# Reading the stationary weights with a step of two elements in a float32r encoder trunk

## The chip, the cores and the metric

The kernel runs on 1 core of one Trainium2 chip. The metric is device microseconds of that core for one execution; shorter is better. The time before is the median of three runs.

## The reference

Two residual layers over one sequence of 256 tokens, 2048 channels, all in float32. Layer 0 mixes tokens by a gated MLP (gMLP), layer 1 by grouped-query attention with 16 heads; after each stands a gated feed-forward with a three-tap convolution. Every part is normed and modulated by a conditioning vector c. Cut to the products that matter here:

```python
mod = silu(c) @ w_ada[i] + b_ada[i]              # 6 vectors of 2048 a layer: "ada"
h = rmsnorm(x) * (1 + sc1) + sh1
# layer 0                                        # layer 1
u, v = split(gelu(h @ w_in))                     # q, k, v = split(h @ w_qkv)
y = (u * spatial(rmsnorm(v))) @ w_out            # y = attention(q, k, v) @ w_o
x = x + gt1 * y
h = rmsnorm(x) * (1 + sc2) + sh2
g, val = split(conv3(h @ w_up))                  # w_up: 2048 x 11264
x = x + gt2 * ((gelu(g) * val) @ w_down)         # w_down: 5632 x 2048
```

## The kernel before

Activations lie transposed: channels on the 128 partitions, the 256 tokens along the free dimension. A float32 product is made of three float32r products: each operand is split into a part hi (its value cast to float32r) and a part lo (the rest), and hi x hi, hi x lo and lo x hi are summed in PSUM (`prod_b`, L204 to 208).

`weight` (L175 to 199 with its inner function) loads up to 128 x 2048 weights into a raw tile by one DMA from SP's queue, casts each half of 1024 columns into a tile hi on ScalarE (L185) and subtracts it into a tile lo on VectorE (L186). It gives back a function `cols(c, n)`, which returns the slices of hi and lo that hold the columns c to c + n. There are five raw, five hi and five lo buffers.

Most products use a weight block of 128 x 128 as the stationary operand (lhsT) and 256 tokens as the moving one, one weight load to each matmul: pu (`w_in`, u half) and po (`w_out`) in layer 0, pw (`w_o`) in layer 1, and in both layers pfa, pfc and pf (`w_up`, in three arrays) and pd (`w_down`). They call `cols` with n = 128. In pu, pfa, pfc and pf the moving operand is a slice of the tiles hhi and hlo (the normed input, all 16 channel blocks in one tile); in po, pw and pd it is a tile fhi or flo of its own for each block. The products pv (`w_in`, v half), pk and pq (`w_qkv`) are turned round: 512 weight columns move, and a block of hhi or hlo is stationary.

The conditioning vectors are made on VectorE alone: 192 column blocks of w_ada, each 1 MB from DRAM, each one multiply-and-sum of 128 x 2048 (L137). A queue deals them out among the weights at a rate set for each stage (`pump`), most of them in layer 0 and in the attention; the feed-forward of layer 1 has none behind its first part.

A scheduler sets the order of instructions on each engine. On the host, `_layout` puts each weight array into DRAM in the order in which it is read: a row of a partition holds the blocks of 128 columns side by side.

Of the kernel before, what the change touches and what calls it, by code (L numbers as in the profile page):

```python
# [15 lines left out]
P = 128  # L16
# [30 lines left out]
def kernel(  # L47
# [21 lines left out]
        return cur["ps"].tile([P, 512], F32, tag=tag or cur["tag"], name=name, bufs=cur["bufs"][tag or cur["tag"]])  # L69

    def phase(stack, name, nf, bufs={"ps": 8}, tag="ps", rt="ps"):
        """pools that live for one mixer: PSUM banks, split activations, scratch"""
        cur["ps"] = stack.enter_context(tc.tile_pool(name=name + "_ps", bufs=1,
                                                     space=bass.MemoryType.PSUM, reuse_waits="tile"))
        cur["bufs"], cur["tag"], cur["rt"] = bufs, tag, rt
        cur["f"] = stack.enter_context(tc.tile_pool(name=name + "_f", bufs=nf, reuse_waits="tile"))
        cur["scr"] = stack.enter_context(tc.tile_pool(name=name, bufs=1, reuse_waits="tile"))
        return cur["scr"]
# [1 line left out]
    def raw_tile(name):  # L80
        return raws.tile([P, 2048], F32, tag="raw", name=name)

# [1 line left out]
    def small(name, shape, src=None):  # L84
        t = const.tile(shape, F32, tag=name, name=name)
        if src is not None:
# [7 lines left out]
    x = const.tile([P, NB, S], F32, tag="x", name="x")  # L94
# [13 lines left out]
    mod = small("mod", [P, DEPTH, 6 * NB])  # L108
    gs = small("gs", [P, DEPTH * 2, NB])

# [1 line left out]
    cond = small("cond", [P, NB])  # L112
    A.activation(cond, cT, AF.Exp, scale=-1.0)
    V.tensor_scalar(out=cond, in0=cond, scalar1=1.0, scalar2=None, op0=ALU.add)
# [14 lines left out]
        A.copy(cond_bc[:, b * S:(b + 1) * S], pb[:, :S])  # L129
    c_st.close()  # L130

# [1 line left out]
    def ada(l, vec, j):  # L133
        m = vec * NB + j
        w = raw_tile(f"ada{l}_{m}")
# [21 lines left out]
        while it not in done:  # L157
            pump_one()

# [1 line left out]
    cnt = [0]  # L161
    pend = []

# [11 lines left out]
    def weight(src, ncol):  # L175
        pump()
        cnt[0] += 1
        w = raw_tile(f"w{cnt[0]}")
        Q.dma_start(w[:, :ncol], src)
        his_, los_ = [], []  # L180
        for c in range(0, ncol, HW):
            n = min(HW, ncol - c)
            hi = his.tile([P, HW], F32R, tag="hi", name=f"hi{cnt[0]}_{c}")
            lo = los.tile([P, HW], F32R, tag="lo", name=f"lo{cnt[0]}_{c}")
            A.copy(hi[:, :n], w[:, c:c + n])  # L185
            V.tensor_tensor(out=lo[:, :n], in0=w[:, c:c + n], in1=hi[:, :n].bitcast(F32), op=ALU.subtract)  # L186
            his_.append(hi)
            los_.append(lo)

        ready = list(pend)  # L190
        pend.clear()
        for fn in ready:
            fn()

        def cols(c, n):
            k, o = divmod(c, HW)
            return his_[k][:, o:o + n], los_[k][:, o:o + n]

        return cols
# [7 lines left out]
        mm(out, whi, xlo, False, False)  # L207
        mm(out, wlo, xhi, False, stop)

# [1 line left out]
    accs = {}  # L211

    def square_into(name, j, src):
# [1 line left out]
            square_(name, j, src)  # L215

    def square_(name, j, src):
        """sum of squares over the blocks of x, two blocks at a time; the last block goes to the tensor engine"""
        if j < NB - 2 and j % 2 == 0:
            return  # L220
        if j < NB - 2:
            src, n = x[:, j - 1:j + 1, :].rearrange("p j t -> p (j t)"), 2 * S
        else:
            n = S
        if j == 1:
            accs[name] = tmp.tile([P, 2 * S], F32, tag="acc", name=f"acc_{name}", bufs=1)
            A.activation(accs[name], src, AF.Square)
            return
        s = tmp.tile([P, 2 * S], F32, tag="sqj", name=f"sq_{name}{j}", bufs=SQB)[:, :n]
        A.activation(s, src, AF.Square)  # L230
        if j < NB - 1:
            V.tensor_tensor(out=accs[name][:, :n], in0=accs[name][:, :n], in1=s, op=ALU.add)
        else:
            a = accs[name]
            accs[name] = (a[:, S:], a[:, :S], s)

    def rstd_bcast(name, keep):
        """1 / rms of every token over all partitions: a PSUM tile, and a copy in SBUF if it is kept for long"""
        pm = bank(f"pm_{name}", cur["rt"])
        r = tmp.tile([P, TC], F32, tag="r", name=f"r_{name}")  # L240
        dg = tmp.tile([P, S], F32, tag="ht", name=f"dg_{name}")
        pr = bank(f"pr_{name}", cur["rt"])
        for i, a in enumerate(accs[name]):
            for t in range(TC):
                T.matmul(pm[:, t:t + 1], lhsT=a[:, t * P:(t + 1) * P], rhs=mean_w, start=i == 0 and t == 0,
                         stop=i == 2, skip_group_check=True)
        with tc.high_priority():
            V.tensor_scalar(out=r, in0=pm[:, :TC], scalar1=EPS, scalar2=None, op0=ALU.add)
            G.tensor_tensor(out=r, in0=r, in1=neghalf[:, :TC], op=ALU.pow)
            for t in range(TC):  # L250
                V.tensor_scalar(out=dg[:, t * P:(t + 1) * P], in0=ident, scalar1=r[:, t:t + 1],
                                scalar2=None, op0=ALU.mult)
                T.matmul(pr[:, t * P:(t + 1) * P], lhsT=ones, rhs=dg[:, t * P:(t + 1) * P], start=True, stop=True)
            if not keep:
                return pr[:, :S]
            R = cur["scr"].tile([P, S], F32, tag="R", name=f"R_{name}", bufs=1)
            A.copy(R, pr[:, :S])
        return R
# [32 lines left out]
            V.scalar_tensor_tensor(out=x[:, j, :], in0=src, scalar=mcol(l, vec, j), in1=x[:, j, :],  # L291
                                   op0=ALU.mult, op1=ALU.add)

# [1 line left out]
    def gmlp(l, rstd):  # L295
        with ExitStack() as st:
            gm = phase(st, "gm", NB)
# [87 lines left out]
    def gqa(l, rstd):  # L385
        with ExitStack() as st:
            at = phase(st, "at", NH, {"pa": 2, "pq": 2, "pb": 4}, "pb", "pq")
# [18 lines left out]
            for kb in range(NB):  # L406
                w = weight(wqkv0_d[kb], 1536)
# [7 lines left out]
                        mm(pk[t][n], hlo[:, kb, ts_], w(n * 512, 512)[0], False, kb == NB - 1)  # L415

            def rope(nm, ps2, cs):
                """un-normalised rotation of four heads and 1/rms of each; ps2: banks per t-chunk"""
                ss = at.tile([P, TC * 4], F32, tag="qss", name=f"ss{cs}", bufs=2)
                rot = [at.tile([P, 512], F32, tag="p", name=f"rot{cs}{t}", bufs=PB) for t in range(TC)]  # L420
                for t in range(TC):
                    src = ps2[t]
                    for h in range(4):
                        s = at.tile([P, P], F32, tag="qsq", name=f"qsq{cs}{t}{h}", bufs=2)
                        A.activation(s, src[:, h * P:(h + 1) * P], AF.Square,
                                     accum_out=ss[:, t * 4 + h:t * 4 + h + 1])
                    s4 = src.rearrange("p (h d) -> p h d", h=4)
                    V.tensor_tensor(out=rot[t].rearrange("p (h d) -> p h d", h=4), in0=s4,
                                    in1=tabs[nm + "c"][:, t:t + 1, :].broadcast_to([P, 4, P]), op=ALU.mult)
                    sw = at.tile([P, 512], F32, tag="sw", name=f"sw{cs}{t}", bufs=1)  # L430
                    s5 = src.rearrange("p (h a c f) -> p h a c f", h=4, a=2, c=2)
                    sw5 = sw.rearrange("p (h a c f) -> p h a c f", h=4, a=2, c=2)
                    t5 = tabs[nm + "s"][:, t, :].rearrange("p (a c f) -> p a c f", a=2, c=2)
                    for c in range(2):
                        V.tensor_tensor(out=sw5[:, :, :, c, :], in0=s5[:, :, :, 1 - c, :],
                                        in1=t5[:, :, c, :].unsqueeze(1).broadcast_to([P, 4, 2, 32]), op=ALU.mult)
                    V.tensor_tensor(out=rot[t], in0=rot[t], in1=sw, op=ALU.add)
                V.tensor_scalar(out=ss, in0=ss, scalar1=1.0 / P, scalar2=EPS, op0=ALU.mult, op1=ALU.add)
                G.tensor_tensor(out=ss, in0=ss, in1=neghalf, op=ALU.pow)
                return rot, ss  # L440
# [91 lines left out]
            for half in range(2):  # L532
                for j2 in range(NB // 2):
                    w = weight(wo_d[half, j2], 2048)
# [16 lines left out]
    def ffn(l, rstd, nxt, defer):  # L551
        with ExitStack() as st:
# [7 lines left out]
                return b[:, :S], b[:, S:]  # L560

            def epilogue(i, src):
                """three-tap convolution along the tokens of both halves, then gelu(g) * val, split"""
                t = ff.tile([P, 2 * S], F32, tag="t", name=f"t{l}_{i}", bufs=2)
                cols = (i, NPAIR + i)
                for a, o, n in zip(src, halves(t), cols):
# [70 lines left out]
            for pi, nk in enumerate(PARTS):  # L637
# [11 lines left out]
                for j in range(NB):  # L649
                    off = base * NB * P + j * nk * P  # L650
                    w = weight(wdn_d[l, :, off:off + nk * P], nk * P)
# [49 lines left out]


def _cols(a, *lead):
    """(..., n*128) -> [128, ..., n]"""
    n = a.shape[-1] // P
    a = a.reshape(*a.shape[:-1], n, P)
    return np.moveaxis(a, -1, 0)


def _nblock(w):  # L710
    """(K, N) -> [N/128][128 k][K/128, 128 n]: the blocks of one column block side by side"""
    K, N = w.shape
    return w.reshape(K // P, P, N // P, P).transpose(2, 1, 0, 3).reshape(N // P, P, -1)


def _rope_tables():
# [11 lines left out]
def _layout(inp):  # L728
    a = {k: np.asarray(v) for k, v in inp.items()}
    o = {}  # L730
# [28 lines left out]
    parts, b = [], 0  # L759
    for nk in PARTS:  # L760
        parts.append(dn[:, b:b + nk].transpose(0, 2, 3, 1, 4).reshape(DEPTH, P, NB * nk * P))
        b += nk
    o["wdn"] = np.concatenate(parts, 2)
    o["ident"] = np.eye(P, dtype=np.float32)
    o["cos"], o["sin"] = _rope_tables()
    return {k: np.ascontiguousarray(v) for k, v in o.items()}
# [23 lines left out]
```

## Time and profile before

| | before |
|---|---|
| median of 3 runs | 2172.94 us (2172.78 to 2173.63) |
| profiled execution, first to last instruction | 2173.2 us |
| mean granted TensorE clock | 0.980 |
| TensorE matmul busy | 2099.9 us (97%), 16328 matmuls |
| TensorE weight load busy | 2037.8 us (94%), 16328 loads |
| VectorE busy | 1706.8 us (79%) |
| ScalarE busy | 1019.5 us (47%) |
| HBM read | 575.99 MB, 266 GB/s over the span |

The profiled execution's span is its own time; it lies 0.3 us over the median of the runs. Records of neighbouring matmuls overlap (a matmul of 256 columns has a record of about 0.28 us), so the time that a matmul takes in a stream is the distance from one start to the next, not the length of its record.

### The profile page before, as it was taken

The numbers are of one execution on the slowest core, as the hardware profiler recorded it, in microseconds if no ns is written. First come the engines' busy times: TensorE is split into PE (matmuls) and PEld (weight loads), VectorE is DVE, ScalarE is ACT, GpSimd is POOL, SyncE is SP. The second block draws the span as 40 slices with busy tenths as digits, with TensorE's granted clock in tenths as the row PEclk, the third lists the DMA queues.
The fourth block names the chain that finished last, engine by engine and source line by source line (L and its number), as shares of the span: only waits on it lengthen the run. The fifth ranks groups of instructions, "written<-read, shape, count | busy, mean of one in ns | idle before, by whom it ended". The sixth has DMA issues, their size and how long they took to land.

```text
span 2173.2 us, 39151 instructions
## 1 busy us (share of the span) xinstructions
PE 2099.9 (97%) x16328; PEld 2037.8 (94%) x16328; DVE 1706.8 (79%) x2291; ACT 1019.5 (47%) x1501; POOL 16.6 (1%) x15
## 2 busy tenths in 40 slices
PE   6889998999999999999999999899999999999997
PEld 4669998999999999999988789899999999999997
DVE  8989888889988989889985677876978566655665
ACT  3343444446544554345455554443653445434542
POOL 0000000000000000000000000000000000000000
PEclk7999999999999999999999999899999999999999
DMA  9999997885798889988976346677558655555542
GB/s 370 405 376 360 343 335 275 338 356 201 282 356 326 324 327 336 335 324 309 338 251 224 119 177 242 218 272 296 192 179 320 229 184 178 192 181 188 174 159 95
DMA packets 85137, 580.62 MB, mean 267 GB/s; under 512 B 9952, under 2 KB 11488, under 8 KB 25056
## 3 DMA queue, kind: packets, MB, share of 16 engines
q1 hardware_dynamic: 84960, 578.12, 71.6%
q8 instruction: 128, 2.10, 0.4%
q14 instruction: 49, 0.40, 0.1%
HBM read 575.99 MB, written 2.10 MB: 266 GB/s over the span
## 4 chain that ended last, share of the span: by engine, by line
PE 54%; issue 36%; DVE 7%; ACT 1%; DMA 1%; POOL 0%; SPq 0%; POOLq 0%; DVEq 0%; ACTq 0%
PE pf L202 18%; PE pd L202 11%; PE po L202 4%; PE pu L202 4%; PE pfc L202 4%; DVE ada L137 4%; PE pw L202 3%; PE pk L202 3%; PE pq L202 3%; DVE lo L186 2%; PE pfa L202 2%; PE pqo L506 1%; PE psc L477 0%; DMA ada<-in_wada 0%; ACT hi L185 0%
## 5 line engine op out<-in xcount | busy, mean ns | idle before, releaser
L185 ACT CAST hi<-w 128x1024 fp32r<-128x1024 f32 x740 | 740.1, 1008 | 929.9 <-PE pf L202 360.7
L186 DVE TENSOR_TENSOR lo<-w,hi 128x1024 fp32r<-128x1024 f32 x740 | 859.6, 1170 | 358.6 <-ACT hi L185 353.1
L202 PE MATMUL pf<-hhi_f,lo 128*128 128x256 f32 x2144 | 606.8, 283 | 0.0
L202 PE MATMUL pf<-hhi_f,hi 128*128 128x256 f32 x2144 | 606.8, 283 | 0.0
L202 PE MATMUL pf<-hlo_f,hi 128*128 128x256 f32 x2144 | 606.8, 283 | 0.0
L137 DVE CUSTOM_DVE_ANT_0 ada<-ada,cond_bc,bada 128x2048 f32<-128x2048 f32 x192 | 449.3, 2346 | 24.2 <-DMA ada<-in_wada 24.0
L202 PEld LDWEIGHTS pf<-hhi_f,hi 128*128 128x128 f32 x2144 | 411.6, 192 | 0.0
L202 PEld LDWEIGHTS pf<-hhi_f,lo 128*128 128x128 f32 x2144 | 411.6, 192 | 0.0
L202 PEld LDWEIGHTS pf<-hlo_f,hi 128*128 128x128 f32 x2144 | 411.6, 192 | 0.0
L202 PE MATMUL pd<-fhi_f,hi 128*128 128x256 f32 x1408 | 392.1, 280 | 0.0
L202 PE MATMUL pd<-flo_f,hi 128*128 128x256 f32 x1408 | 391.6, 279 | 0.0
L202 PE MATMUL pd<-fhi_f,lo 128*128 128x256 f32 x1408 | 391.2, 279 | 0.0
L202 PEld LDWEIGHTS pd<-fhi_f,lo 128*128 128x128 f32 x1408 | 264.1, 188 | 0.0
L202 PEld LDWEIGHTS pd<-fhi_f,hi 128*128 128x128 f32 x1408 | 263.6, 188 | 0.0
L202 PEld LDWEIGHTS pd<-flo_f,hi 128*128 128x128 f32 x1408 | 263.1, 187 | 0.0
L202 PE MATMUL pfc<-hhi_f,hi 128*128 128x256 f32 x448 | 126.1, 283 | 0.0
L202 PE MATMUL pfc<-hlo_f,hi 128*128 128x256 f32 x448 | 126.1, 283 | 0.0
L202 PE MATMUL pfc<-hhi_f,lo 128*128 128x256 f32 x448 | 125.5, 283 | 0.0
L570 DVE SCALAR_TENSOR_TENSOR t<-pf,cw,t 128x255 f32<-128x255 f32 x240 | 101.7, 474 | 0.0
L202 PEld LDWEIGHTS pfc<-hhi_f,hi 128*128 128x128 f32 x448 | 85.8, 192 | 0.0
L202 PEld LDWEIGHTS pfc<-hlo_f,hi 128*128 128x128 f32 x448 | 85.8, 192 | 0.0
L202 PEld LDWEIGHTS pfc<-hhi_f,lo 128*128 128x128 f32 x448 | 85.4, 192 | 0.0
(187 smaller groups left out, 2844.6 us busy)
## 6 DMA issues: line engine op xcount, KB each, us to landing
ada<-in_wada SPq DMA_DIRECT2D x192, 1024.0 KB, 6.6
w<-in_wup SPq DMA_DIRECT2D x134, 1024.0 KB, 4.8
w<-in_wdn SPq DMA_DIRECT2D x64, 1024.0 KB, 4.9
w<-in_wup SPq DMA_DIRECT2D x48, 896.0 KB, 5.5
w<-in_wdn SPq DMA_DIRECT2D x32, 768.0 KB, 4.7
w<-in_wv SPq DMA_DIRECT2D x16, 1024.0 KB, 7.1
w<-in_wu SPq DMA_DIRECT2D x16, 1024.0 KB, 7.1
w<-in_wout SPq DMA_DIRECT2D x16, 1024.0 KB, 5.3
```

Source lines behind the costliest of these rows:

```text
L137: V.tensor_tensor_reduce(out=w, in0=w, in1=cond_bc, op0=ALU.mult, op1=ALU.add, scale=1.0, scalar=bada[:, l, m:m + 1], accum_out=mod[:, l, ...
L185: A.copy(hi[:, :n], w[:, c:c + n])
L186: V.tensor_tensor(out=lo[:, :n], in0=w[:, c:c + n], in1=hi[:, :n].bitcast(F32), op=ALU.subtract)
L202: T.matmul(out, lhsT=a, rhs=b, start=start, stop=stop, skip_group_check=True)
L506: T.matmul(po, lhsT=va[:, kc, g * P:(g + 1) * P], rhs=ps_[h][:, kc, :], start=kc == 0, stop=kc == TC - 1)
L570: V.scalar_tensor_tensor(out=o[:, to], in0=a[:, frm], scalar=cw[:, l, tap, n:n + 1], in1=o[:, to], op0=ALU.mult, op1=ALU.add)
```

## The change

Two neighbouring blocks of 128 columns are laid in DRAM by turns, column 0 of the first, column 0 of the second, column 1 of the first, and so on, in all arrays whose blocks are stationary. The DMA, the cast and the subtraction treat the row as before. `cols`, asked for one block (n = 128), returns every second element of the 256 that hold the pair. Where 512 columns move (`in_wv`, `in_wqkv0`, `in_wqkv1`) nothing changes. In the built program 14976 of the 16328 weight loads read with a step of two elements instead of one; the instructions, their order and their waits are otherwise the same on every engine. Comments that went away are left out here.

```diff
@@ weight @@
         def cols(c, n):
             k, o = divmod(c, HW)
+            if n == P:
+                o, q = o // (2 * P) * (2 * P), o // P % 2
+                return [t[:, o:o + 2 * P].rearrange("p (n q) -> p q n", q=2)[:, q, :] for t in (his_[k], los_[k])]
             return his_[k][:, o:o + n], los_[k][:, o:o + n]
@@ host @@
+def _pairs(w):
+    return w.reshape(*w.shape[:-1], -1, 2, P).swapaxes(-1, -2).reshape(w.shape)
...
@@ _layout @@
     o["wdn"] = np.concatenate(parts, 2)
+    for k in ("wu", "wout", "wo", "wup0", "wup1", "wup2", "wdn"):
+        o[k] = _pairs(o[k])
```

## Rows read from the trace of the kernel before

**Rows 1.** The page: span, busy time by engine, clock in 40 slices.

```profile
span 2173.2 us, 39151 instructions
...
PE 2099.9 (97%) x16328; PEld 2037.8 (94%) x16328; DVE 1706.8 (79%) x2291; ACT 1019.5 (47%) x1501; POOL 16.6 (1%) x15
...
PEclk7999999999999999999999999899999999999999
```

**Rows 2.** Chain of waits, in order of time: start us, length us, what, matmuls.

```profile
252.47 87.52 PE po L202 x743
...
561.11 90.45 PE pd L202 x768
651.56 184.32 PE pf L202 x1536
```

**Rows 3.** Timeline of PE, 512 columns moving: start us, record us, what.

```profile
1150.43 0.39 PE L202 MATMUL pk<-lo,hhi_b 128*128 128x512 f32 x1
...
1150.88 0.39 PE L202 MATMUL pk<-lo,hhi_b 128*128 128x512 f32 x1
1151.11 0.39 PE L202 MATMUL pk<-hi,hhi_b 128*128 128x512 f32 x1
```

**Rows 4.** PE's timeline in a stretch at half clock, and its window (PEclk: granted clock).

```profile
353.88 0.41 PE L202 MATMUL pfa<-hlo_f,hi 128*128 128x256 f32 x1
354.09 0.41 PE L202 MATMUL pfa<-hhi_f,lo 128*128 128x256 f32 x1
...
354.73 0.41 PE L202 MATMUL pfa<-hhi_f,lo 128*128 128x256 f32 x1
...
core 0: us, PE busy (x) PEld busy (x) DVE busy (x) ACT busy (x) POOL busy (x), PEclk, DMA share, GB/s
353.70:354.90 1.20, 1.20 (x7) 1.20 (x7) 1.02 (x4) 0.72 (x2) 0.00 (x0) 0.50 0.00 0
```

**Rows 5.** Timeline of weight loads near the end, before float32 matmuls of few columns.

```profile
2159.88 0.53 PEld L245 LDWEIGHTS pm_fin<-mean_w,acc_fin 128*128 128x128 f32 x4
2160.79 0.52 PEld L245 LDWEIGHTS pm_fin<-mean_w,sq_fin 128*128 128x128 f32 x4 [0.38 <-ACT sq_fin L230]
2162.75 0.52 PEld L253 LDWEIGHTS pr_fin<-dg_fin,ones 128*128 128x128 f32 x4 [1.44 <-DVE dg_fin L251]
```

**Rows 6.** Groups of instructions, one of three alike for each tile: xcount, busy us, mean ns.

```profile
L202 PE MATMUL pf<-hhi_f,lo 128*128 128x256 f32 x2144 | 606.8, 283 | 0.0
...
L202 PE MATMUL pd<-fhi_f,hi 128*128 128x256 f32 x1408 | 392.1, 280 | 0.0
...
L202 PE MATMUL pfc<-hhi_f,hi 128*128 128x256 f32 x448 | 126.1, 283 | 0.0
...
L202 PE MATMUL pw<-fhi_o,hi 128*128 128x256 f32 x256 | 72.5, 283 | 0.0
...
L202 PE MATMUL pu<-hlo_a,hi 128*128 128x256 f32 x256 | 72.3, 283 | 0.0
...
L202 PE MATMUL po<-fhi_y,hi 128*128 128x256 f32 x256 | 71.6, 280 | 0.0
...
L202 PE MATMUL pfa<-hlo_f,hi 128*128 128x256 f32 x224 | 64.1, 288 | 0.0
```

**Rows 7.** Windows (columns as in rows 4): pf, pf and pd of layer 0, pf of layer 1.

```profile
474.70:561.10 86.40, 86.40 (x723) 86.40 (x722) 79.22 (x126) 53.85 (x87) 0.00 (x0) 1.00 0.64 234
...
651.60:835.90 184.30, 184.30 (x1538) 184.30 (x1537) 166.14 (x218) 91.21 (x126) 0.00 (x0) 1.00 0.87 324
...
1041.50:1105.00 63.50, 63.50 (x542) 63.50 (x541) 61.23 (x82) 30.01 (x41) 0.00 (x0) 1.00 0.94 355
...
1686.00:1870.00 184.00, 184.00 (x1538) 184.00 (x1538) 112.94 (x153) 88.47 (x120) 0.00 (x0) 1.00 0.55 195
```

**Rows 8.** Waits between 651.6 and 835.9 us: total us, times, longest.

```profile
DVE lo L186 <- ACT hi L185: 17.8, 24, 1.3
...
ACT hi L185 <- PE pf L202: 90.9, 64, 1.9
```

## The prediction

> **What bounds the kernel now.** I read the shares of the engines first [rows 1]. TensorE (PE) is busy 97% of the span, VectorE (DVE) 79%, and the granted clock is full (the digit 9) in all but a few of the forty slices. A busy PE says nothing of its peak, so the next view is the chain of work, where one piece is one unbroken run of matmuls on one tile [rows 2]. From it comes the time per matmul, the pitch: 184.32 us / 1536 = 120.0 ns for pf, whose moving operands are hhi and hlo, and 90.45 / 768 = 117.8 ns for pd, with fhi and flo moving; po has 87.52 / 743 = 117.8 ns. Each of these matmuls streams 256 columns and has a weight load of its own. 256 columns at 2.4 GHz are 106.7 ns, so 13.3 ns (pf) or 11.1 ns (pd) of each pitch are not column time.
>
> Where do they come from? The same surplus stands at twice the columns: four matmuls of 512 columns start within 0.68 us [rows 3], 0.68 / 3 = 226.7 ns apart, against 213.3 ns of columns. So it goes with the weight load, not with the columns. At half clock it is gone: in a stretch with a granted clock of 0.50, matmuls of 256 columns start 0.21 us apart [rows 4]; four pitches, from the first of five to the last, take 0.85 us, 212.5 ns each, and 256 columns at 1.2 GHz are 213.3 ns. The load alone is seen where a float32 matmul behind it has one column, or 128: four loads take 0.53, 0.52 or 0.52 us from the start of the first to the end of the last [rows 5]. One record is 0.19 us, so a load comes every (0.523 - 0.19) / 3 = 111 ns. That is under 120 ns: the load by itself does not set the pitch. It and the stream together do, at full clock alone, by an amount that differs between tiles with the same shapes and types. My reading, not shown by a row: both read SBUF at once, and some reads meet.
>
> **The change part by part.** Loads read with a step of two: three matmuls per weight block, so three times the counts of [rows 6]: pf 2144, pd 1408, pfc 448, pu 256, pfa 224, and po and pw 256 each. That is 3 x 4992 = 14,976 of 16,328 loads, in two groups: hhi/hlo moving (pf, pfc, pu, pfa) 3 x 3072 = 9216, and fhi/flo or their like moving (pd, po, pw) 3 x 1920 = 5760. The loads of pv, pk and pq take their weights from hhi and hlo and stay as they are. Every engine's instructions, their order and their waits are the same in the two built programs, and the DMAs move the same bytes into the same tiles; hi and lo are made element by element, so ScalarE's cast and VectorE's subtraction cost the same. The host's regrouping of the arrays is not device time. What is left is one price: a load that steps 8 bytes a column instead of 4, beside a stream that steps 4 bytes a column.
>
> No row shows a load with a step, so I bound it. Below: the surplus goes, 106.7 ns by column time, or 111 ns by the load alone [rows 5]. Above: the load passes over 1024 bytes instead of 512, and the surplus doubles with them, to 133.3 and 128.9 ns. A load held to half its rate would be worse: 2 x 111 = 222 ns a pitch.
>
> I take 111 ns. Reason: the load needs about 256 cycles for 128 columns (2 cycles a column: [rows 4] leave no room for more at half clock), so it reads 2 bytes a cycle against the stream's 4, and the two slide past each other through the whole load. A step of two makes both advance 4 bytes a cycle. Two streams of equal speed meet at the same place always or never, and one that has to wait once falls out of step with the other and meets it no more. That the surplus already depends on which tiles meet [rows 2] speaks for meetings that depend on place, rather than for a fixed fee per load.
>
> The sum: 9216 x (120.0 - 111) = 82.9 us and 5760 x (117.8 - 111) = 39.2 us, 122 us of PE time. Of it, layer 0 holds (pu 768, pfa 336, pfc 672, pf 3216: 4992 x 9 = 44.9; pd 2112, po 768: 2880 x 6.8 = 19.6) 64.5 us, and layer 1 with pw 57.6 us.
>
> What hides there is VectorE. In layer 0 it is nearly as long as PE [rows 7]: 166.14 of 184.30 us in the largest pf stretch, 79.22 of 86.40 and, in a pd stretch, 61.23 of 63.50. At 111 ns these would be 170.5, 79.9 and 59.8 us of PE: VectorE level with PE or past it. Its idle time in the first of these is 17.8 us behind ScalarE's cast, which itself waits 90.9 us for PE to free the hi tiles [rows 8]: a faster PE frees them sooner, so VectorE can close up, but not to the last microsecond. I keep two thirds of layer 0's gain, 43 us. In layer 1 VectorE has 112.94 of 184.00 us [rows 7], so nearly all of its 57.6 us counts; I take 55. Together 98 us. The profiled execution has 2173.2 us [rows 1], 0.3 us over the median of the runs, so the result is 2172.9 - 98 = **2075 us**.
>
> **The rivals.**
> (1) Nothing moves, 2173 us. The surplus may be a fixed fee of a load beside a full-rate stream, whatever the step: for it speaks that pf stays at 120.0 ns over 1536 matmuls and that 512 columns pay the same 13.3 ns; against it, that pd pays less. [...]
> (2) Slower: the meetings grow with the bytes that a load passes over. Then 9216 x 13.3 + 5760 x 11.1 = 187 us are added, on the path throughout since VectorE only gets more room: 2360 us. For it speaks that the surplus belongs to the load and that a load's length in bytes is what doubles; against it, that it needs meetings by count of places and not by phase. It decides against my forecast from any pitch over 120 and 117.8 ns on. If instead a strided load ran at half rate, 14,976 x about 100 ns = 1.5 ms would be added; nothing in the rows points there beyond the lack of a row.
> (3) The change does not do what it says: the built program has the step in 14,976 loads, so this can't be.
> (4) PE gets faster but VectorE or the queue of transfers eats it: only layer 1 gains, 2118 us. It is the upper part of my forecast's range.
>
> **How the numbers follow.** My forecast, faster with 2015 to 2130 us: 0.50. Its low end is the whole surplus gone in layer 1 (4224 x 13.3 + 2880 x 11.1 = 88 us) and two thirds of it in layer 0 (0.67 x 98 = 65 us): 2020 us, and a little less for layer 0 keeping more; its high end is half of the 98 us (2124 us). Rival (1): 0.22. Rival (2): 0.28, of which 0.06 lies beyond a doubling. The range that leaves out less than 2 in 10 must reach to the doubling: 2015 to 2370 us. What can be told from no change in this kernel is about 0.2%, 4.3 us; faster 0.50, same 0.22, slower 0.28.
>
> **What would show it.** In the chain after, the pieces of pf and pd give the pitch directly: 109 to 113 ns for both by my forecast, 120.0 and 117.8 by (1), about 133 and 129 by (2). pk's 226.7 ns must stand in every case. If I am right, VectorE's share in layer 0 goes to 95% and PE shows gaps there behind VectorE's lo tiles, while layer 1 shows none. A pitch of pf and pd that still differ by 2 ns would say that the step does not remove the meetings; a pitch over 120 ns that I have the sign of the phase argument wrong.

## The result and the profile after

The changed kernel is slower by 0.6%: 2186.1 us (2184.4 to 2189.1, four runs) against 2173.3 us (2172.8 to 2173.7, four runs), ratio 1.0062 with a 95% interval of 1.0047 to 1.0076. That is 12.8 us more, where 98 us less were forecast.

The page of the changed kernel, the lines that answer to [rows 1]:

```profile
span 2183.6 us, 39151 instructions
...
PE 2111.5 (97%) x16328; PEld 2049.4 (94%) x16328; DVE 1708.2 (78%) x2291; ACT 1021.2 (47%) x1501; POOL 16.6 (1%) x15
...
PEclk9999999999999999999999999999999999999998
```

Nothing but PE's time has moved: matmuls 2111.5 us for 2099.9, loads 2049.4 for 2037.8; VectorE and ScalarE are as they were to within 2 us. The spans differ by 10.4 us and not by 12.8. In the timed runs of the changed kernel the time is 1.9 us longer than the span (2185.5 against 2183.6 us in the profiled one), so by this measure the profiled execution before, with its span of 2173.2 us, was some 2 us slower than its median, and not the 0.3 us that a comparison of its span with the median gives. In its first slice the granted clock was lower (digit 7; 0.75 over the first 54 us, against 1.00 in the changed kernel), which this one has not; that the difference comes from there is likely and not shown.

The chain of waits of the changed kernel: start us, length us, what, matmuls; it answers to [rows 2]:

```profile
250.62 89.17 PE po L206 x743
...
561.46 92.16 PE pd L206 x768
653.62 184.32 PE pf L206 x1536
...
1324.01 66.49 PE pw L206 x554
```

The longest piece of pw in the kernel before:

```profile
1318.59 51.13 PE pw L202 x434
```

Read as a pitch: pf 184.32 / 1536 = 120.0 ns, to the last digit what it was. pd 92.16 / 768 = 120.0 ns, before 117.8; po 89.17 / 743 = 120.0 ns, before 117.8; pw 66.49 / 554 = 120.0 ns, before 51.13 / 434 = 117.8. So the tiles that had a small bonus over the others lost it, and those without one lost nothing: 5760 x 2.22 ns = 12.8 us, which is the whole result.

What the step does not touch has stayed. Matmuls with 512 moving columns and a contiguous load, as in [rows 3]:

```profile
1151.31 0.39 PE L206 MATMUL pk<-lo,hhi_b 128*128 128x512 f32 x1
1151.54 0.39 PE L206 MATMUL pk<-hi,hhi_b 128*128 128x512 f32 x1
1151.76 0.39 PE L206 MATMUL pk<-lo,hhi_b 128*128 128x512 f32 x1
1151.99 0.39 PE L206 MATMUL pk<-hi,hhi_b 128*128 128x512 f32 x1
```

0.68 us for three pitches again. And the pf stretch of layer 0, with columns as in [rows 4], answering to the second line of [rows 7]:

```profile
653.60:837.90 184.30, 184.30 (x1538) 184.30 (x1537) 166.04 (x218) 91.41 (x126) 0.00 (x0) 1.00 0.86 323
```

1538 matmuls in 184.3 us, VectorE 166.04 us: the same line but for some hundredths. VectorE never came into play, since PE did not get faster.

### The profile page after: what moved, and what is told of

It is laid out like the page before. It is cut to its first block, busy times and chain, and to the rows that moved or that the text cites. A ratio compares the mean times of both kernels' runs of the same rounds, so it can differ in the third digit from the quotient of the medians.

```text
span 2183.6 us, 39151 instructions
## 1 busy us (share of the span) xinstructions
PE 2111.5 (97%) x16328; PEld 2049.4 (94%) x16328; DVE 1708.2 (78%) x2291; ACT 1021.2 (47%) x1501; POOL 16.6 (1%) x15
## 4 chain that ended last, share of the span: by engine, by line
PE 55%; issue 36%; DVE 7%; ACT 1%; POOL 0%; DMA 0%; SPq 0%; POOLq 0%; DVEq 0%; ACTq 0%
PE pf L206 18%; PE pd L206 11%; PE po L206 4%; PE pw L206 4%; PE pu L206 4%; PE pfc L206 4%; DVE ada L137 3%; PE pk L206 3%; PE pq L206 3%; DVE lo L186 2%; PE pfa L206 2%; PE pqo L510 1%; PE psc L481 0%; PE psc L503 0%; ACT hi L185 0%
## 5 line engine op out<-in xcount | busy, mean ns | idle before, releaser
L206 PEld LDWEIGHTS pf<-hhi_f,hi 128*128 128x128 f32 x2144 | 420.2, 196 | 0.0
L206 PEld LDWEIGHTS pf<-hlo_f,hi 128*128 128x128 f32 x2144 | 420.2, 196 | 0.0
L206 PEld LDWEIGHTS pf<-hhi_f,lo 128*128 128x128 f32 x2144 | 420.2, 196 | 0.0
L206 PE MATMUL pd<-flo_f,hi 128*128 128x256 f32 x1408 | 397.2, 283 | 0.0
L206 PE MATMUL pd<-fhi_f,lo 128*128 128x256 f32 x1408 | 396.9, 283 | 0.0
L206 PEld LDWEIGHTS pd<-flo_f,hi 128*128 128x128 f32 x1408 | 278.4, 198 | 0.0
L206 PEld LDWEIGHTS pd<-fhi_f,lo 128*128 128x128 f32 x1408 | 278.2, 198 | 0.0
L206 PEld LDWEIGHTS pd<-fhi_f,hi 128*128 128x128 f32 x1408 | 278.0, 198 | 0.0
```

Source lines behind the costliest of these rows:

```text
L206: T.matmul(out, lhsT=a, rhs=b, start=start, stop=stop, skip_group_check=True)
```

## The experiments

**Where the loss is: the step in a part of the arrays.** Two kernels, each with half of the change; both in the form

```diff
-    def weight(src, ncol):
+    def weight(src, ncol, two=False):
...
-            if n == P:
+            if two:
```

with `True` passed, and the host's regrouping done, for `wout`, `wo` and `wdn` in the one, and for `wu`, `wup0`, `wup1` and `wup2` in the other.

> The step of two only in the arrays whose products have fhi/flo moving (po, pw, pd); the others read contiguously. Reading of the trace after: all of the loss is in these 5760 matmuls, 2.2 ns each = 12.7 us. If so: 2173.3 + 12.7 = 2186 us, pf at 120.0 ns, pd at 120.0 ns. If the loss is elsewhere (waits, transfers): between 2173 and 2186 us with pd at 117.8.

Measured: 2186.5 us, ratio 1.0063 (1.0048 to 1.0078). The chain:

```profile
562.16 92.16 PE pd L206 x768
654.32 184.31 PE pf L206 x1536
```

> The step of two only in the arrays whose products have hhi/hlo moving (pu, pfa, pfc, pf); po, pw and pd read contiguously. If the step costs nothing where the pitch already is 120.0 ns: 2173 us, pf 120.0 and pd 117.8 ns. If part of the loss came from these 9216 loads: up to 2186 us.

Measured: 2172.7 us, ratio 0.9999 (0.9990 to 1.0009). The chain:

```profile
558.86 90.45 PE pd L206 x768
649.32 184.31 PE pf L206 x1536
```

So 9216 strided loads cost nothing, and the other 5760 cost all of it. Both pf pieces, one contiguous and one strided, have 120.0 ns.

**What the bonus of pd, po and pw was.** hhi and hlo start 64 bytes past a multiple of 128 in SBUF, as raw, hi and lo do; fhi and flo start on a multiple of 128. Two kernels without any step move tiles by unused strips of 64 bytes, e3_shift_all by one ahead of all these tiles, e4_align_h by one ahead of hhi and one behind hlo:

```diff
     cond_bc = small("cond_bc", [P, D])
+    small("pad", [P, 16])                     # e3_shift_all
...
+    padh = ctx.enter_context(tc.tile_pool(name="padh", bufs=1)).tile([P, 16], F32, ...)   # e4_align_h
     hbuf = ctx.enter_context(tc.tile_pool(name="hbuf", bufs=1))
+    padt = ctx.enter_context(tc.tile_pool(name="padt", bufs=1)).tile([P, 16], F32, ...)   # e4_align_h
     tmp = ctx.enter_context(tc.tile_pool(name="tmp", bufs=2))
```

> The kernel before (no step) with 64 bytes left free ahead of the raw tiles, so that raw, hi, lo, hhi, hlo, fhi and flo all lie 64 bytes further on. hhi and hlo then start on a multiple of 128 bytes and fhi and flo 64 bytes past one; before it is the other way round. Theory A (the start of the moving tile within 128 bytes sets the pitch): pf 117.8, pd 120.0 ns, 9216 x -2.2 + 5760 x 2.2 = -7.7 us: 2165.6 us. Theory B (the place of the moving tile against that of the weights, which is as before): pf 120.0, pd 117.8, 2173 us. Theory C (a tile of its own for each block against slices of one tile): pf 120.0, pd 117.8, 2173 us.

Measured: 2171.0 us, ratio 0.9992 (0.9983 to 1.0001). In the chain pf has 184.32 us for 1536 and pd 90.45 us for 768, as before. Theory A falls: moving all tiles together changes nothing for these two. One product did change, pw:

```profile
1316.02 49.20 PE pw L203 x434
```

49.20 / 434 = 113.4 ns, where the kernel before has 117.8 with the same distance between the tiles.

> The kernel before (no step) with 64 bytes left free ahead of hhi and 64 behind hlo: hhi and hlo start on a multiple of 128 bytes, as fhi and flo do; raw, hi and lo stay. Theories A and B: pf goes to 117.8 ns as well, 9216 x 2.2 = 20.3 us less: 2153 us. Theory C: pf stays at 120.0 ns, 2173 us.

Measured: 2138.6 us (2130.6 to 2142.3), ratio 0.984 (0.982 to 0.986), more than forecast. The chain:

```profile
553.78 90.45 PE pd L204 x768
644.23 180.91 PE pf L204 x1536
...
1305.38 62.82 PE pw L204 x554
```

pf is at 180.91 / 1536 = 117.8 ns: moved by 64 bytes against the weights, slices of one large tile get the same bonus. Theory C falls, and theory B, that the place of the moving tile against that of the weights matters, stands. With the two strips fhi and flo have moved by 128 bytes against the weights, and pw has 62.82 / 554 = 113.4 ns. The other part that B did not foresee is pd in layer 1. Windows of 54 us of pd in layer 0 and in layer 1 (columns as in [rows 4]):

```profile
561.00:615.00 54.00, 54.00 (x461) 54.00 (x460) 49.88 (x63) 27.60 (x41) 0.00 (x0) 1.00 0.83 318
1890.00:1944.00 54.00, 54.00 (x479) 54.00 (x478) 29.07 (x30) 21.03 (x20) 0.00 (x0) 1.00 0.57 195
```

The same code on the same places runs 461 matmuls in the one and 479 in the other (a few are cut by the edges). The timeline there has nine pitches in 1.02 us:

```profile
1899.75 0.28 PE L204 MATMUL pd<-fhi_f,hi 128*128 128x256 f32 x1
...
1900.77 0.28 PE L204 MATMUL pd<-fhi_f,hi 128*128 128x256 f32 x1
```

113.3 ns. So there is more than one rhythm for one placement.

**The step at the better place.** The changed kernel with the same two strips of 64 bytes:

> The changed kernel (step of two) with hhi and hlo 64 bytes further on, as in e4_align_h; fhi, flo, raw, hi and lo as in the kernel before, within 128 bytes. Theory D (with a step of two the load's 13.3 ns are paid wherever the two tiles lie): pf and pd 120.0 ns, as in the changed kernel, 2186 us plus what pv, pk and pq lose (e4_align_h has 233.3 ns there for 226.7: 1352 x 6.7 ns = 9 us): about 2195 us. Theory E (the step only turns round which places are good): pf at 117.8 ns or less, pd 120.0, 2174 us or less.

Measured: 2194.8 us, ratio 1.010 (1.0085 to 1.0115). The chain:

```profile
477.21 87.60 PE pf L208 x720
564.81 92.17 PE pd L208 x768
656.98 184.32 PE pf L208 x1536
```

120.0 ns in the last two, where the contiguous kernel on the same places has 117.8, and 87.60 / 720 = 121.7 ns in the first. Theory E falls: with a step of two this place brings no gain. It is not without effect, though: pfc, two pieces of pf in layer 0 and one in layer 1 have 121.7 ns. These 3888 matmuls account for some 6.5 us; the expectation had the whole 9 us over the changed kernel from pv, pk and pq, so that the total came out right is in part luck.

**The weights moved instead.** Strips of 64 bytes ahead of the raw tiles and ahead of hhi, no step:

> The kernel before (no step) with raw, hi and lo 64 bytes further on; hhi, hlo, fhi and flo as before within 128 bytes. Theory B (place of the moving tile against that of the weights): pf 117.8 ns or less, pd, po and pw 120.0 ns, and 233.3 ns for pv, pk and pq: -20.3 + 12.7 + 9 us, about 2174 us. Theory A' (the moving tile's own place together with something that e3_shift_all moved as well): pf 120.0, pd 117.8, 2173 us.

Measured: 2160.5 us, ratio 0.994 (0.993 to 0.996). The chain:

```profile
555.53 91.13 PE pd L204 x768
646.66 180.91 PE pf L204 x1536
```

pf has 117.8 ns with hhi at its old place within 128 bytes, so it is the distance that counts; pd has 118.7 and not 120.0. Theory B is right in kind, but the effect does not repeat every 128 bytes: pd's distance here is 128 bytes off a multiple of 256, and pf's in the kernel before was a multiple of 256.

**Larger steps.** `cols` with a group of g blocks by turns, g = 4 in pu, pd and the pairs of pf, g = 8 in po, pw and the first pf tiles:

```diff
+            if g > 1:
+                o, q = o // (g * P) * (g * P), o // P % g
+                return [t[:, o:o + g * P].rearrange("p (n q) -> p q n", q=g)[:, q, :] for t in (his_[k], los_[k])]
```

> The kernel before with larger steps: 4 elements (16 bytes) in pu, pd and the pairs of pf, 8 elements (32 bytes) in po, pw and the first seven tiles of pf; pfa and pfc read contiguously. Theory F (each column of a load is fetched alone and pays nothing for its distance; the 13.3 ns are the most that a load can cost its neighbour): all of them 120.0 ns, 2186 us. [...]

Measured: 3666.8 us, ratio 1.688 (1.685 to 1.690). Theory F, 120.0 ns and 2186 us, falls. The chain:

```profile
335.19 184.75 PE po L205 x767
...
822.05 179.21 PE pd L205 x768
1001.26 358.39 PE pf L205 x1536
```

pd and pf with a step of four: 233.3 ns; po with a step of eight: 240.9 ns. That is twice the 117.8 and 120.0 ns of pd and pf in the kernel before, and 12,960 loads x about 115 ns are the 1.49 ms. That such a load sets the pitch alone is an estimate from these pitches; no run has it beside a narrow stream. The cliff lies between a step of two (120.0 ns in the changed kernel) and one of four (233.3 ns).

**The load nearly alone.** The kernels with and without the step, the second and third product of a block cut to 64 columns:

```diff
         mm(out, whi, xhi, start, False)
-        mm(out, whi, xlo, False, False)
-        mm(out, wlo, xhi, False, stop)
+        mm(out[:, :NARROW], whi, xlo[:, :NARROW], False, False)
+        mm(out[:, :NARROW], wlo, xhi[:, :NARROW], False, stop)
```

> The changed kernel (step of two), but of the three products of a block the second and third stream 64 token columns instead of 256 and leave the other 192 out (the first keeps all). With 64 columns (27 ns) the load sets the pitch, so this shows a load of step two nearly alone. Theory D (the load itself is as long as a contiguous one; the 13.3 ns come from the stream beside it): 107 to 112 ns from a narrow matmul to the next, as in e11_narrow. Theory H (a load of step two itself takes 120 ns, so that the place of the tiles cannot matter any more): 118 to 120 ns.

> The same with the kernel before (contiguous loads): 107 to 112 ns from a narrow matmul to the next, by both theories; it is what e10_narrow_step is held against. Leaves out the same 192 columns of the second and third product.

One run of each; the totals, 3368.9 and 3356.9 us, are of no use here, since the granted clock is 0.50 throughout pfc, pf and pd. pu still ran at full clock. Loads of pu in the timeline, contiguous first:

```profile
200.14 0.19 PEld L203 LDWEIGHTS pu<-hhi_a,lo 128*128 128x128 f32 x1
200.24 0.19 PEld L203 LDWEIGHTS pu<-hhi_a,hi 128*128 128x128 f32 x1
200.35 0.19 PEld L203 LDWEIGHTS pu<-hlo_a,hi 128*128 128x128 f32 x1
200.48 0.19 PEld L203 LDWEIGHTS pu<-hhi_a,lo 128*128 128x128 f32 x1
```

and with the step of two:

```profile
200.19 0.20 PEld L207 LDWEIGHTS pu<-hhi_a,lo 128*128 128x128 f32 x1
200.31 0.20 PEld L207 LDWEIGHTS pu<-hhi_a,hi 128*128 128x128 f32 x1
200.43 0.20 PEld L207 LDWEIGHTS pu<-hlo_a,hi 128*128 128x128 f32 x1
200.56 0.20 PEld L207 LDWEIGHTS pu<-hhi_a,lo 128*128 128x128 f32 x1
```

Contiguous loads follow after 0.10, 0.11 and 0.13 us: the third has the wide stream of 256 columns beside it, the other two narrow ones. With the step it is 0.12, 0.12 and 0.13 us, nearly the same whatever streams beside. Means over pu, worked out from the starts of all its loads in the two traces (single pauses over 160 ns left out): contiguous 108.7 and 111.0 ns beside a narrow stream and 120.3 beside the wide one; with the step 118.5, 117.8 and 119.9 ns. The chain has the mean over the whole of pu and of po, also at full clock, contiguous and with the step:

```profile
173.32 76.08 PE pu L203 x672
249.40 84.22 PE po L203 x743
```

```profile
173.16 79.71 PE pu L207 x672
252.87 89.15 PE po L207 x743
```

113.2 against 118.6 ns in pu, 113.4 against 120.0 in po. At half clock there is no difference; pd of either kernel (window, granted clock 0.50):

```profile
714.50:878.30 163.80, 163.80 (x769) 163.80 (x770) 77.59 (x81) 39.17 (x52) 0.00 (x0) 0.50 0.51 186
```

```profile
722.90:886.70 163.80, 163.80 (x769) 163.80 (x770) 77.49 (x81) 39.22 (x52) 0.00 (x0) 0.50 0.51 187
```

Theory H stands: at full clock a load of step two takes 118 to 119 ns beside a narrow stream, some 7 to 10 ns more than a contiguous one.

**Other places, no step.** One strip of 32 bytes, one of 160, and two of 192 bytes in the form of e4_align_h:

> The kernel before (no step) with hhi and hlo 32 bytes further on and fhi and flo as well: hhi then lies 32 bytes past the place of the weights within 128 bytes, fhi 96 bytes past it. Theory B with a grain of 64 bytes: pf stays at 120.0 ns or pd at 117.8, one of both; with a grain of 32 bytes or less, both move. Between 2130 and 2200 us.

Measured: 2159.8 us (2157.8 to 2170.0), ratio 0.995 (0.993 to 0.998); in the chain pf has 179.20 us for 1536, 116.7 ns, and pd 92.15 for 768, 120.0 ns. Both moved, so steps of 32 bytes in the distance already count.

> The kernel before (no step) with hhi and hlo 160 bytes and fhi and flo 224 bytes past the weights' place within 256 bytes: two places not yet seen. If the place within 128 bytes decides, as e8_place32 (32 and 96): pf 117.1, pd 120.0 ns, 2160 us. If the place within 256 bytes decides, other pitches, none over 120 ns on the mean: 2120 to 2185 us.

Measured: 2160.4 us, ratio 0.995 (0.993 to 0.997); pf 180.22 us, 117.3 ns, pd 90.88 us, 118.3 ns. pd is not at the 120.0 ns that the same place within 128 bytes gave it, so the effect does not repeat every 128 bytes.

The distances from the weights to the moving tile in the built programs, modulo 256 bytes, with the pitch of the chain's pieces in layer 0: 0 (pf before) 120.0 ns, 32 and 96 (e8_place32) 116.7 and 120.0, 64 (pd before) 117.8, 128 (pd of e6_shift_w) 118.7, 160 and 224 (e12_place160) 117.3 and 118.3, 192 (pd of e4_align_h) 117.8. One distance can have other pitches as well, as pw in e3_shift_all and the next kernel show.

> The kernel before (no step) with hhi and hlo as well as fhi and flo 192 bytes past the weights' place within 256 bytes, where e4_align_h had fhi and flo (pd at 113.3 ns in layer 1, 117.8 in layer 0). Theory I (the place within 256 bytes decides): pf goes to 113.3 ns in some stretches at least, 9216 x 6.7 = 61 us if in all: 2100 to 2138 us. Theory B as it stood (only the place within 128 bytes decides): as e4_align_h, 2138 us, pf 117.8.

Measured: 2115.4 us (2108.2 to 2139.8), ratio 0.972 (0.971 to 0.974): the fastest kernel here, ahead of both. Its profile is of the slowest of its five executions, 2139.8 us, and shows in one execution both rhythms of pf at the same places:

```profile
461.70 81.60 PE pf L204 x720
543.29 89.47 PE pd L204 x768
632.77 180.91 PE pf L204 x1536
```

81.60 / 720 = 113.3 ns and 180.91 / 1536 = 117.8 ns. Theory I is borne out by the first of them. The change of rhythm lies inside the pd piece between them, in mid-run, and the largest pf piece of layer 1 has the slower one too (windows, columns as in [rows 4]; 25 us are 223 matmuls and then 214):

```profile
545.00:570.00 25.00, 25.00 (x223) 25.00 (x223) 23.14 (x38) 14.85 (x26) 0.00 (x0) 1.00 0.74 275
572.00:597.00 25.00, 25.00 (x214) 25.00 (x214) 24.62 (x28) 10.95 (x14) 0.00 (x0) 1.00 0.93 361
1672.00:1852.00 180.00, 180.00 (x1531) 180.00 (x1530) 112.22 (x155) 89.83 (x124) 0.00 (x0) 1.00 0.53 188
```

The other four executions probably had 113.3 ns in more stretches; their times (2108 to 2117 us) agree with that, but no profile shows it.

## Why the prediction was wrong

The bottleneck was read rightly: PE's pitch in the products with one load to each matmul, and nothing else moved. The counts (9216 and 5760 loads) and the two pitches were right as well, and pk's 226.7 ns stood, as said. The 106.7 ns for 256 columns, from which the surplus is counted, are what this case gives: pk's 226.7 ns for 512 columns less pf's 120.0 ns for 256, and half of the 213.3 ns that pf and pd take at a granted clock of 0.50 in e10_narrow_step and e11_narrow. That the surplus over column time depends on the place of the moving tile against the weights is shown by e4_align_h and e6_shift_w; that reads of the load and of the stream meet is the reading that fits this, and no run shows it directly.

What failed is "I take 111 ns". The 111 ns of [rows 5] are the price of a contiguous load alone, and the text carried it over, without a row, to a load of step two, as if that one took no longer. The narrow kernels show that at full clock this does not hold: 118 to 119 ns with the step against 109 to 111 ns without, beside a narrow stream. By these numbers pd had no room to keep its old pitch of 117.8 ns, and pf about 2 ns to win. In the changed kernel all of them ran at 120.0 ns: pf, which was there already, lost nothing; pd, po and pw came up to it from 117.8. What makes 120.0 of 118 to 119 beside the wide stream is not shown. The phase argument, that two streams of equal speed fall out of step, was the author's estimate; no run shows it, and it stays open: the longer load left it next to nothing to win, and the 121.7 ns in e5_align_h_step say that with the step, too, the place still counts.

The bounds were too simple in the same place. The upper one, that the surplus doubles with the bytes passed over (133.3 ns), did not come. The worse case named under rival (2), a load at half its rate, was given "nothing in the rows points there"; it is what a step of four does, 233.3 ns against the 222 ns worked out, and e7_steps48's 12,960 loads cost 1.49 ms where that sentence had 1.5 ms for 14,976.

Rival (1), nothing moves, came nearest: right for 9216 of the loads, for which the step is free (e2_step_h: 2172.7 us, ratio 0.9999). That a load pays the same whatever the step does not hold in general: beside a narrow stream one with a step of two takes 6 to 9% more (118 to 119 ns for 109 to 111), and with a step of four the pitch is 233.3 ns. Nor is the surplus the same at every place: hhi and hlo moved by 64 bytes against the weights took pf from 120.0 to 117.8 ns (e4_align_h).

Rival (2) had the sign, and its size was off: +187 us for +12.8. The term that was mis-sized is 9216 x 13.3 + 5760 x 11.1 ns; measured it is 9216 x 0 + 5760 x 2.2. The range, 2015 to 2370 us, held the time; the point and the sign of the forecast were wrong.

## What to carry to other kernels

Price a changed access pattern of a load by the load alone, with a narrow stream beside it, before arguing on how two streams meet: here the steady pitch with 256 columns moving stayed above it, 113.3 ns at the least for a load of 109 to 111 ns and 119.9 for one of 118 to 119, and this floor, risen close to the old pitch, looked like no effect in 9216 matmuls (pf at 120.0 ns before and after) and like a loss in the 5760 that had a bonus (pd, po and pw from 117.8 to 120.0 ns). Where float32r blocks of 128 x 128 are loaded for 256 moving columns each, the distance in SBUF between the moving tile and the weights is worth trying: two unused strips of 64 or of 192 bytes each took 1.6% and 2.8% off this kernel with no instruction changed. Keep a stationary float32 operand's step at one or two elements: pd and pf had 117.8 and 120.0 ns without a step, both had 120.0 with a step of two, and 233.3 with one of four.

## What was not expected of the hardware

The pitch of one and the same form has several steady values at full clock, 120.0, 117.8 and 113.3 ns among them, the last two at the same place in one execution (e9_place192, e4_align_h). What brings a stretch into one or the other stays open. That VectorE and the transfers have less to do in layer 1, where pd of e4_align_h came to 113.3 ns (VectorE 29.07 of 54 us and a DMA share of 0.57, against 49.88 us and 0.83 in layer 0), is not enough: in e9_place192 it is layer 0 that has 113.3 ns and layer 1's largest pf piece that has 117.8. It also stays open what sets the 13.3 ns that a matmul of 256 or 512 columns has over 106.7 or 213.3 ns at the kernel's old place (120.0 and 226.7 ns), and why a load of step two takes 118 to 119 ns at full clock for 109 to 111, when at half clock the pitch is 213.3 ns with either.

The products with 512 moving columns went the other way. With hhi moved by 64 bytes (e4_align_h) pk's timeline has six pitches in 1.40 us, 233.3 ns for 226.7 before, so one place does not suit both uses of hhi:

```profile
1140.02 0.39 PE L204 MATMUL pk<-hi,hhi_b 128*128 128x512 f32 x1
...
1141.42 0.86 PE L204 MATMUL pk<-hi,hlo_b 128*128 128x512 f32 x3
```

And with two products of three cut to 64 columns the granted clock fell to half (0.50) in nearly all of the feed-forward, where a pitch of 213.3 ns took the place of 117.8 to 120.0, so that a kernel with less work for PE took 3357 us instead of 2173. The page of the narrow kernel without the step, the clock in 40 slices:

```profile
PEclk9999555555555555555579985555555555555555
```
